# Products of quarters: two outputs computed in place, in the tile of the sum whose last use they are

## The chip, the cores and the metric

The kernel runs on one core of a Trainium2 chip. The metric is the device time of one execution in microseconds (us). Before the change it is 3474.56 us, the median of three runs (3472.7 to 3475.61). Engines are named as in the profile: PE (TensorE), DVE (VectorE), ACT (ScalarE), POOL (GpSimd) and SP (SyncE, which here only issues DMAs).

## The reference

A two-layer backbone over 1024 latent tokens and 256 context tokens, D = 1024. The change touches only how some input projections are computed:

```
qa, ka, va, za, qb, kb, vb, ob, zb, g = _split_cols(h @ w_in, AB_SIZES)   # layer 0
...
    qb, kb = _axial_rope(qb), _axial_rope(kb)                             # latent tokens only
...
q, f_fwd, f_bwd, i, z = _split_cols(h @ w_in, C_SIZES)                    # layer 1
...
(o.reshape(o.shape[:2] + (HG_VW,)) * jax.nn.silu(z)) @ w_out
```

In layer 0 the products concerned are h @ w_in for three pairs of heads: q of heads 0 and 1, k of heads 0 and 1, k of heads 2 and 3 (with the rotation `_axial_rope` for the latent tokens). In layer 1 they are the columns of i (the values) and of z, of which silu(z) is kept.

## The kernel before, in words

**Products of quarters.** `q_seven` (from line 961) multiplies a matrix h (quarters 11, 12, 21, 22: two halves of the tokens by two halves of D) with a 2 x 2 block of weight columns by seven products of quarters in place of eight, in this order: 11 and 12 (`q_two`, line 953), s1, s2, s3, 22, s4, where s1 to s4 use sums of quarters of h. Each quarter product is done in fp32r with a split into a high and a low part, so each 128x256 block takes 12 matmuls (lines 127, 128, 129: high by high, low weight by high, high weight by low). Two running sums live in SBUF tiles: u (names qu, q_keep, line 941) and v (names qv). u is started by the product 11 (copied by ACT, line 957), enlarged by s2 (line 969) and s3 (line 974), and last used in the product 22. v is made from s1 and u (line 971), and last used in the product s4.

**The four outputs.** `q_out` (lines 948 to 951) takes a new output tile, lets DVE add or subtract a product in PSUM to or from the sum (line 950, one instruction per unit), and gives the tile to a sink. There are four calls: the output of the product 12 (reads u), of s3 (reads v), of 22 (last use of u) and of s4 (last use of v). The output tiles rotate: in layer 0 two buffers named ev (shared with the projections before and after the stage), in layer 1 three buffers named qo.

**Sinks.** In layer 0 the sink rotates q and k in place (`rope`, lines 1018 to 1021: four DVE instructions per unit, with a scratch tile qs; units of context tokens are not rotated) and stores the tile to DRAM (line 981, a DMA issued by POOL; md is the place in DRAM). In layer 1 the values go to DRAM at once (line 981, into vd), and for z ACT computes a sigmoid into qg (line 991), DVE multiplies in place (line 992) and POOL issues the store (line 994, into zd).

**Units and buffers.** A product is cut into units, each with a PSUM bank (names sa, mm, tr; eight banks in all). Layer 0: half = 5 blocks of 128 tokens, units of 1, 2 and 2 blocks (128x256, 128x512, 128x512), two sets of u and one set of v. Layer 1: half = 4, two units of 128x512, one set of u and one of v. Layer 0 has three blocks of columns through `q_seven` (the first two have their `q_two` done ahead, `a_ahead`, from line 1028), layer 1 has seven.

**Weights.** `q_form` forms sums of raw weight quarters on DVE (line 899) and splits them: ACT casts the high part (wh, line 74), DVE subtracts for the low part (wl, line 75); each of wh and wl has four buffers. After the stage of layer 0 the neighbourhood attention begins: `na_qk` takes weights through the same buffers and lines, projects (lines 127 to 129 into mm), copies the bank to an ev tile (ACT, line 565) and goes on from there. Its second set of weights, for `na_z`, is in SBUF space that the tiles of the stage (u, v, qs among them) had.

**What sets the order.** A scheduler orders the instructions of each engine ahead of time. On the chip each engine runs its list in order; where a tile is not free yet, the instruction that wants it waits, and all behind it on the engine wait too. In the whole-run trace the stage of layer 0 lies at about 284 to 450 us, that of layer 1 at about 1915 to 2190 us.

Of the kernel before, what the change touches and what calls it, by code (L numbers as in the profile page):

```python
# [9 lines left out]
F32 = mybir.dt.float32  # L10
# [3 lines left out]
ALU = mybir.AluOpType  # L14
# [4 lines left out]
P = 128  # L19
# [27 lines left out]
class Prog:  # L47
# [897 lines left out]
    def q_keep(self, pool, tag, m):  # L945
        return self.t(pool, [P, m * 256], F32, f"{tag}{m}", self.qn * sum(x[1] == m for x in self.units))

    def q_out(self, sink, r, c, u, in0, in1, op):
        o = self.t(self.qo[0], [P, 512], F32, *self.qo[1:])[:, 0 : u[1] * 256]
        self.nc.vector.tensor_tensor(out=o, in0=in0, in1=in1, op=op)  # L950
        sink(c, r * self.half + u[0], u[1], o)

# [9 lines left out]
    def q_seven(self, raw, S, sink, pool, u=None, tr=False):  # L962
        tt = self.nc.vector.tensor_tensor
        u = u or self.q_two(raw, S, sink, pool, tr)
        v, m5 = {}, {}
        for i, ps in self.q_product("s1", S, self.q_form(raw, "11", "12"), tr):
            m5[i] = ps
        for i, ps in self.q_product("s2", S, self.q_form(raw, "11", "22"), tr):
            tt(out=u[i], in0=u[i], in1=ps, op=ALU.add)
            v[i] = self.t(pool, [P, i[1] * 256], F32, f"qv{i[1]}", sum(x[1] == i[1] for x in self.units))  # L970
            tt(out=v[i], in0=m5[i], in1=u[i], op=ALU.subtract)
        for i, ps in self.q_product("s3", S, self.q_form(raw, "12", "22"), tr):
            self.q_out(sink, 1, 1, i, v[i], ps, ALU.subtract)
            tt(out=u[i], in0=u[i], in1=ps, op=ALU.add)
        for i, ps in self.q_product("22", S, self.q_form(raw, "11", "21"), tr):
            self.q_out(sink, 1, 0, i, u[i], ps, ALU.add)
        for i, ps in self.q_product("s4", S, self.q_form(raw, "22"), tr):
            self.q_out(sink, 0, 1, i, v[i], ps, ALU.add)

    def q_store(self, dst, t, m, o):  # L980
        self.nc.gpsimd.dma_start(
# [686 lines left out]
```

## Time and profile before

| | |
|---|---|
| median of three runs | 3474.56 us (3472.7 to 3475.61) |
| the profiled execution | 3477.65 us; span in its trace 3475.9 us; mean granted TensorE clock 0.996 |
| instructions in the span | 63362 |
| DMA | 359.62 MB, mean 103 GB/s |
| chain that ended last, by engine | PE 88%, issue 4%, DMA 2%, DVE 2%, ACT 1%, POOL 1% |

The span is the stretch from the first to the last profiled instruction; the execution's time has 1.75 us more around it. "Busy" of PE counts the time in which at least one matmul is in flight: a 128x256 matmul is shown with 0.28 us, but one starts every 0.12 us, so PE's idle time is read from the distance of starts, not from the busy share. A row of a timeline has the start, the duration, the engine, the line, the operation and the tiles, and in brackets the idle time of the engine just before it and what ended it. A row of waits has who waited for whom, the total in us, how many times, and the longest.

### The profile page before, as it was taken

How to read it: one execution, taken by the hardware profiler on the slowest of the kernel's cores; microseconds unless marked ns; L12 is line 12 of the kernel's file. 1: busy time of each engine (PE TensorE's matmuls, PEld its weight loads, DVE VectorE, ACT ScalarE, POOL GpSimd, SP SyncE). 2: the span in 40 equal slices, each digit the busy share in tenths (PEclk: the TensorE clock that was granted, in tenths of full speed). 3: DMA queues.
4: the chain of work that ended last, by engine and by line, in shares of the span. 5: the costliest groups of instructions: out<-in, count | busy, mean ns of one | idle time of the engine just before them, and what ended most of it. 6: DMA issues, size and time to landing. Idle time of an engine off the chain costs nothing.

```text
span 3475.9 us, 63362 instructions
## 1 busy us (share of the span) xinstructions
PE 3433.5 (99%) x23790; PEld 3111.0 (90%) x23790; DVE 2393.0 (69%) x5876; ACT 1554.2 (45%) x3560; POOL 508.8 (15%) x843
## 2 busy tenths in 40 slices
PE   8999999999999999999999999999999999999999
PEld 6899999999999999988879998889999999999887
DVE  7569857766666654666668766577777777777855
ACT  6532135555545534566536323444444444444431
POOL 3211111222222211211212111000000000000010
PEclk9999999999999999999999999999999999999999
DMA  8542422332222234455475332212111111121345
GB/s 256 165 158 84 124 83 54 91 87 69 81 82 79 75 99 152 128 172 159 131 238 171 101 104 97 82 31 62 62 47 52 58 58 49 52 61 53 113 149 166
DMA packets 354131, 359.62 MB, mean 103 GB/s; under 512 B 30312, under 2 KB 298792, under 8 KB 353696
## 3 DMA queue, kind: packets, MB, share of 16 engines
q1 hardware_dynamic: 309760, 246.28, 24.0%
q0 software_dynamic: 43920, 109.16, 9.2%
q8 instruction: 188, 3.08, 0.4%
q14 instruction: 119, 0.97, 0.1%
q10 hardware_dynamic: 144, 0.13, 0.0%
HBM read 271.90 MB, written 83.42 MB: 102 GB/s over the span
## 4 chain that ended last, share of the span: by engine, by line
PE 88%; issue 4%; DMA 2%; DVE 2%; ACT 1%; POOL 1%; SPq 0%; POOLq 0%; DVEq 0%; ACTq 0%
PE mm L127 15%; PE mm L128 15%; PE mm L129 15%; PE s L1144 6%; PE mm L757 3%; PE mm L759 3%; PE mm L758 3%; PE acc L709 2%; PE tr L689 2%; PE sa L127 2%; PE sa L129 2%; PE sa L128 2%; PE acc L492 2%; PE s L499 2%; PE s L1190 1%
## 5 line engine op out<-in xcount | busy, mean ns | idle before, releaser
L128 PE MATMUL mm<-wl,hh 128*128 128x256 f32 x2200 | 633.0, 288 | 4.0 <-DVE wl L75 3.7
L127 PE MATMUL mm<-wh,hh 128*128 128x256 f32 x2200 | 632.4, 288 | 4.3 <-DVE ev L950 2.7
L129 PE MATMUL mm<-wh,hl 128*128 128x256 f32 x2200 | 632.2, 288 | 0.2 <-DVE hl L75 0.2
L129 PE MATMUL mm<-hh,wl 128*128 128x512 f32 (+1 forms) x1372 | 499.7, 364 | 0.0
L128 PE MATMUL mm<-hl,wh 128*128 128x512 f32 (+1 forms) x1372 | 495.6, 361 | 0.0
L127 PE MATMUL mm<-hh,wh 128*128 128x512 f32 (+1 forms) x1372 | 495.2, 361 | 0.0
L127 PEld LDWEIGHTS mm<-wh,hh 128*128 128x128 f32 x2200 | 420.5, 191 | 12.3 <-issue 6.9
L128 PEld LDWEIGHTS mm<-wl,hh 128*128 128x128 f32 x2200 | 420.9, 191 | 9.4 <-DVE wl L75 5.0
L129 PEld LDWEIGHTS mm<-wh,hl 128*128 128x128 f32 x2200 | 420.5, 191 | 4.1 <-issue 0.8
L74 ACT CAST wh<-wraw 128x512 fp32r<-128x512 f32 x292 | 180.0, 621 | 280.1 <-PE mm L128 147.2
L128 PEld LDWEIGHTS mm<-hl,wh 128*128 128x128 f32 x1372 | 259.3, 189 | 32.2
L127 PEld LDWEIGHTS mm<-hh,wh 128*128 128x128 f32 x1372 | 259.4, 189 | 32.1
L129 PEld LDWEIGHTS mm<-hh,wl 128*128 128x128 f32 x1372 | 259.2, 189 | 32.0 <-issue 0.2
L1135 ACT COPY gksel<-gK 128x512 f32<-128x512 f32 x224 | 148.3, 663 | 275.7 <-PE s L1144 264.6
L75 DVE TENSOR_TENSOR wl<-wraw,wh 128x512 fp32r<-128x512 f32 x292 | 198.5, 688 | 50.5 <-ACT wh L74 47.9
L1144 PE MATMUL s<-gQ,gksel 128*128 128x128 f32 x1536 | 202.1, 276 | 0.0
L1144 PEld LDWEIGHTS s<-gQ,gksel 128*128 128x128 f32 x1536 | 192.6, 191 | 5.8
L757 PE MATMUL mm<-woh,yh 128*128 128x512 f32 (+1 forms) x420 | 168.9, 402 | 4.1 <-issue 2.3
L758 PE MATMUL mm<-wol,yh 128*128 128x512 f32 (+1 forms) x420 | 167.1, 399 | 0.0
L759 PE MATMUL mm<-woh,yl 128*128 128x512 f32 (+1 forms) x420 | 166.2, 397 | 0.1
L1165 DVE TENSOR_TENSOR gQ<-gQ,gT 128x256 f32<-128x256 f32 x384 | 143.9, 417 | 21.3 <-PE s L1144 21.3
L74 ACT CAST wh<-b 128x512 fp32r<-128x512 f32 x122 | 75.7, 620 | 182.3 <-PE sa L129 56.4
(551 smaller groups left out, 8240.4 us busy)
## 6 DMA issues: line engine op xcount, KB each, us to landing
wraw<-in_wc_dram SPq DMA_DIRECT2D x130, 256.0 KB
wraw<-yd SPq DMA_DIRECT2D x128, 256.0 KB
wraw<-in_wab_dram SPq DMA_DIRECT2D x98, 256.0 KB
md<-ev POOLq DMA_DIRECT2D x94, 256.0 KB, 2.7
adar<-in_wada_dram POOLq DMA_DIRECT2D x32, 512.0 KB, 5.0
b<-in_wc_dram SPq DMA_DIRECT2D x62, 256.0 KB
adar<-in_wada_dram SPq DMA_DIRECT2D x16, 512.0 KB
wraw<-in_wab_dram SPq DMA_DIRECT2D x64, 128.0 KB
```

The lines of the kernel that those rows point to most:

```text
L74: nc.scalar.copy(hi, x)
L75: nc.vector.tensor_tensor(out=lo, in0=x, in1=hi.bitcast(F32), op=ALU.subtract)
L127: mm(ps, lhsT=lh(k), rhs=rh(k), start=(first and k == 0), stop=False)
L128: mm(ps, lhsT=lh(k), rhs=rl(k), start=False, stop=False)
L129: mm(ps, lhsT=ll(k), rhs=rh(k), start=False, stop=(last and k == nk - 1))
L492: nc.tensor.matmul(num, lhsT=qc[:, j, :], rhs=C[d][:, j, :], start=False, stop=(j == 1))
L757: mm(ps, lhsT=yh[:, k, :], rhs=w.h(k)[:, cols], start=(k == 0), stop=False)
L758: mm(ps, lhsT=yh[:, k, :], rhs=w.l(k)[:, cols], start=False, stop=False)
L759: mm(ps, lhsT=yl[:, k, :], rhs=w.h(k)[:, cols], start=False, stop=(k == 7))
L1135: nc.scalar.copy(ksel.rearrange("p (b s i) -> p b s i", s=2, i=h), pick(K))
L1144: nc.tensor.matmul(pa[:, c, :].rearrange("p (b s i) -> p b s i", s=2, i=h), lhsT=ksel[:, c * P : (c + 1) * P], rhs=qp[:, c * nbc : (c + 1) ...
L1165: nc.vector.tensor_tensor(out=t[:, i, :, s, :], in0=t[:, i, :, s, :], in1=bc(tot), op=ALU.mult)
```

## The change

```diff
-    def q_out(self, sink, r, c, u, in0, in1, op):
-        o = self.t(self.qo[0], [P, 512], F32, *self.qo[1:])[:, 0 : u[1] * 256]
+    def q_out(self, sink, r, c, u, in0, in1, op, o=None):
+        if o is None:
+            o = self.t(self.qo[0], [P, 512], F32, *self.qo[1:])[:, 0 : u[1] * 256]
         self.nc.vector.tensor_tensor(out=o, in0=in0, in1=in1, op=op)
         sink(c, r * self.half + u[0], u[1], o)
...
         for i, ps in self.q_product("22", S, self.q_form(raw, "11", "21"), tr):
-            self.q_out(sink, 1, 0, i, u[i], ps, ALU.add)
+            self.q_out(sink, 1, 0, i, u[i], ps, ALU.add, u[i])
         for i, ps in self.q_product("s4", S, self.q_form(raw, "22"), tr):
-            self.q_out(sink, 0, 1, i, v[i], ps, ALU.add)
+            self.q_out(sink, 0, 1, i, v[i], ps, ALU.add, v[i])
```

The outputs of the products 22 and s4 no longer take an ev (layer 0) or qo (layer 1) tile: DVE writes them into the tile of u or v, and the rotation, the sigmoid's product and the store work on that tile. The outputs of 12 and s3 are as before. No instruction is added or removed; but half of the takers of ev and qo are gone, a tile of u or v is free again only when its store has landed, and the scheduler, which sees these other waits, orders the stage of layer 0 anew. In layer 1 the order is the same, with other tile names. All lines from 949 on have a number higher by one in the changed kernel (950 becomes 951, and so on).

**Place 1, DVE in the stage of layer 0, around the output of the product 22 of the first block.** Names: qu_515 is the third unit of u of that block, mm_3838 (before) and mm_3836 (after) is the PSUM bank with its product 22, qv_578 and qv_580 are units of v, ev are output tiles, wl the low parts of weights, mrope the table of the rotation. Before:

```order
L1020 TENSOR_TENSOR ev_3797<-ev_3797,qs_3799 128x2x64
L1021 TENSOR_TENSOR ev_3797<-ev_3797,qs_3799 128x2x64
L1018 TENSOR_TENSOR qs_3832<-ev_3830,mrope_2103 128x512
L1019 TENSOR_TENSOR ev_3830<-ev_3830,mrope_2103 128x512
L75 TENSOR_TENSOR wl_4133<-b_622_3969,wh_4134 128x512
L1020 TENSOR_TENSOR ev_3830<-ev_3830,qs_3832 128x4x64
L1021 TENSOR_TENSOR ev_3830<-ev_3830,qs_3832 128x4x64
L75 TENSOR_TENSOR wl_4138<-b_623_3971,wh_4139 128x512
L969 TENSOR_TENSOR qu_538_3357<-qu_538_3357,tr_4060 128x256
L950 TENSOR_TENSOR ev_3863<-qu_515_3231,mm_3838 128x512
L950 TENSOR_TENSOR ev_3887<-qv_576_3621,sa_3874 128x256
L1018 TENSOR_TENSOR qs_3889<-ev_3887,mrope_2103 128x256
```

After, on the same engine at the same place:

```order
L1019 TENSOR_TENSOR qs_3798<-qu_511_3177,mrope_2103 128x256
L951 TENSOR_TENSOR qv_578_3649<-qv_578_3649,sa_3891 128x512
L1020 TENSOR_TENSOR ev_3736<-ev_3736,mrope_2103 128x512
L951 TENSOR_TENSOR ev_3770<-qv_580_3677,tr_3745 128x512
L975 TENSOR_TENSOR qu_515_3231<-qu_515_3231,tr_3745 128x512
L75 TENSOR_TENSOR wl_4045<-wraw_3955,wh_4046 128x512
L1020 TENSOR_TENSOR qu_511_3177<-qu_511_3177,mrope_2103 128x256
L75 TENSOR_TENSOR wl_4050<-wraw_3957,wh_4051 128x512
L1021 TENSOR_TENSOR ev_3736<-ev_3736,qs_3738 128x4x64
L1022 TENSOR_TENSOR ev_3736<-ev_3736,qs_3738 128x4x64
L951 TENSOR_TENSOR qv_580_3677<-qv_580_3677,sa_3923 128x512
L951 TENSOR_TENSOR qu_515_3231<-qu_515_3231,mm_3836 128x512
```

The row that reads the product 22 out of the bank mm (third unit) stood behind the rotations of the units before it and behind the weights of the next block's s3 (wl_4133, wl_4138); now it stands ahead of both, right behind the weights of s2 (wl_4045, wl_4050).

**Place 2, PE at the end of the stage of layer 0.** mm_5086 (before) and mm_5068 (after) are the first projection of `na_qk`, mm_5143 (after) its second; wh_5053/wl_5052 to wh_5074/wl_5073 (before) and wh_5035/wl_5034 to wh_5056/wl_5055 (after) are its four pieces of weights. Before, the rows from the tenth matmul of the first projection on:

```order
L127 MATMUL mm_5086<-wh_5060,hh_128 128x256
L128 MATMUL mm_5086<-wl_5059,hh_128 128x256
L129 MATMUL mm_5086<-wh_5060,hl_129 128x256
L127 MATMUL mm_5086<-wh_5067,hh_128 128x256
L128 MATMUL mm_5086<-wl_5066,hh_128 128x256
L129 MATMUL mm_5086<-wh_5067,hl_129 128x256
L127 MATMUL mm_5086<-wh_5067,hh_128 128x256
L128 MATMUL mm_5086<-wl_5066,hh_128 128x256
L129 MATMUL mm_5086<-wh_5067,hl_129 128x256
L127 MATMUL mm_5086<-wh_5074,hh_128 128x256
L128 MATMUL mm_5086<-wl_5073,hh_128 128x256
L129 MATMUL mm_5086<-wh_5074,hl_129 128x256
```

After, the rows from the 18th matmul after s4 on (ahead of them 12 of mm_5068 and 5 of mm_5143, all with the first two pieces of weights):

```order
L129 MATMUL mm_5143<-wh_5035,hl_129 128x256
L127 MATMUL mm_5143<-wh_5042,hh_128 128x256
L128 MATMUL mm_5143<-wl_5041,hh_128 128x256
L127 MATMUL mm_5068<-wh_5049,hh_128 128x256
L129 MATMUL mm_5143<-wh_5042,hl_129 128x256
L127 MATMUL mm_5143<-wh_5042,hh_128 128x256
L128 MATMUL mm_5143<-wl_5041,hh_128 128x256
L129 MATMUL mm_5143<-wh_5042,hl_129 128x256
L127 MATMUL mm_5143<-wh_5049,hh_128 128x256
L128 MATMUL mm_5068<-wl_5048,hh_128 128x256
L129 MATMUL mm_5068<-wh_5049,hl_129 128x256
L127 MATMUL mm_5068<-wh_5049,hh_128 128x256
```

The second projection is begun ahead of the end of the first: the low part of the third piece of weights was wanted by the 14th matmul after s4 and is now wanted by the 27th.

**Place 3, ACT at the same end.** wh_5462 (before) and wh_5444 (after) is the first weight tile in SBUF space that the stage gives back; ev_5135 and ev_5117 are the copies of the first projection of `na_qk`. Before:

```order
L74 CAST wh_5074<-wraw_5075 128x512
L74 CAST wh_5462<-wraw_5463 128x512
L74 CAST wh_5468<-wraw_5469 128x512
L565 COPY ev_5135<-mm_5086 128x512
L569 ACTIVATE aqn_5137<-ev_5135 128x512
```

After:

```order
L74 CAST wh_5056<-wraw_5057 128x512
L565 COPY ev_5117<-mm_5068 128x512
L74 CAST wh_5444<-wraw_5445 128x512
L74 CAST wh_5450<-wraw_5451 128x512
L569 ACTIVATE aqn_5119<-ev_5117 128x512
```

The copy that frees the bank of the first projection now stands ahead of the cast into space of the stage, instead of behind it. That cast waited for the last rotation (line 1021); now it waits for the landing of the last store of v, too.

## The prediction

> **What bounds the kernel now.** I read the page first, for the engine that is always busy and for what makes it wait; then the stretches of the two stages; then the waits inside the first; then the rows around them.
>
> ```profile
> PE 3433.5 (99%) x23790; PEld 3111.0 (90%) x23790; DVE 2393.0 (69%) x5876; ACT 1554.2 (45%) x3560; POOL 508.8 (15%) x843
> L127 PE MATMUL mm<-wh,hh 128*128 128x256 f32 x2200 | 632.4, 288 | 4.3 <-DVE ev L950 2.7
> ```
>
> PE bounds the run, so only a change of PE's waits or clock moves the time. One of its few waits is on line 950, which the change edits. The stretches (their columns: us, then busy us and count of PE, PEld, DVE, ACT and POOL, the granted clock, DMA share, GB/s):
>
> ```profile
> 316.00:360.00 44.00, 41.62 (x347) 41.19 (x347) 38.44 (x79) 7.46 (x12) 7.98 (x12) 1.00 0.40 120
> 360.00:405.00 45.00, 45.00 (x381) 45.00 (x379) 39.44 (x82) 9.37 (x16) 8.02 (x12) 1.00 0.24 77
> 405.00:450.00 45.00, 39.82 (x315) 39.44 (x314) 33.56 (x66) 6.08 (x11) 8.87 (x14) 0.93 0.50 153
> 1915.00:1990.00 75.00, 75.00 (x480) 68.13 (x479) 55.94 (x90) 25.95 (x42) 9.00 (x14) 1.00 0.31 102
> ```
>
> In layer 0 (first three rows) PE has holes, and in the third row its clock is below 1. In layer 1 (last row) it has neither: there the change can cost, but not gain. In layer 0 the waits say who:
>
> ```profile
> DVE ev L950 <- DMA md<-ev: 16.2, 10, 3.1
> PE mm L127 <- DVE ev L950: 4.8, 2, 2.7
> PE mm L128 <- DVE wl L75: 2.7, 2, 2.5
> ```
>
> DVE stands still ten times, 16.2 us in all, because both ev tiles are still being stored. PE waits twice for line 950 (a PSUM bank not read out) and once at length for a low part of weights, which DVE makes too. The three holes of PE, each with the row before it and the row that ends it:
>
> ```profile
> 353.80 0.28 PE L129 MATMUL tr<-wh,s2l 128*128 128x256 f32 x1
> 356.24 0.36 PE L127 MATMUL mm<-wh,s2h 128*128 128x256 f32 x1 [2.16 <-DVE ev L950]
> 435.47 0.28 PE L127 MATMUL mm<-wh,hh 128*128 128x256 f32 x1
> 438.27 0.38 PE L128 MATMUL mm<-wl,hh 128*128 128x256 f32 x1 [2.52 <-DVE wl L75]
> 441.72 0.28 PE L129 MATMUL mm<-wh,hl 128*128 128x256 f32 x1
> 444.66 0.55 PE L127 MATMUL mm<-wh,hh 128*128 128x256 f32 x1 [2.66 <-DVE ev L950]
> ```
>
> **The sum, term by term.** A 128x256 matmul starts 0.12 us after the one before where nothing waits, so a hole costs the distance of starts less 0.12. Rows from DVE's timeline and from the chain (start, duration, engine, line) give the causes:
>
> ```profile
> 338.48 0.42 DVE L1018 TENSOR_TENSOR qs<-ev,mrope 128x256 f32<-128x256 f32 x1
> 351.47 0.29 DVE L1020 TENSOR_TENSOR ev<-ev,qs 128x128 f32<-128x128 f32 x1
> 351.67 0.29 DVE L1021 TENSOR_TENSOR ev<-ev,qs 128x128 f32<-128x128 f32 x1
> 354.14 0.42 DVE L1021 TENSOR_TENSOR ev<-ev,qs 128x256 f32<-128x256 f32 x1
> 354.48 0.68 DVE L75 TENSOR_TENSOR wl<-b,wh 128x512 fp32r<-128x512 f32 x1
> 355.41 0.68 DVE L950 TENSOR_TENSOR ev<-qu,mm 128x512 f32<-128x512 f32 x1
> 436.92 0.69 DVE L950 TENSOR_TENSOR ev<-qu,sa 128x512 f32<-128x512 f32 x1 [2.77 <-DMA md<-ev]
> 437.53 0.69 DVE L75 TENSOR_TENSOR wl<-wraw,wh 128x512 fp32r<-128x512 f32 x1
> ```
>
> ```profile
> 441.24 2.56 DMA md<-ev
> 443.82 0.70 DVE ev L950
> 445.21 0.21 PE mm L128
> 450.54 0.21 PE mm L129
> 452.22 0.12 PE mm L127
> ```
>
> *Hole 1, 356.24 - 353.80 - 0.12 = 2.32 us.* PE wants the bank mm; line 950 reads it out only at 355.41, though DVE did not wait: it had other rows first. In the new order (place 1) the row with mm_3836 stands nearer. From the row of 338.48, which both orders have, to that row there are now 16 rows of 512 columns (0.61 us apart, as 436.92 and 437.53), 8 that are 256 wide or two halves of a 512 rotation (0.34 apart, as 354.14 and 354.48), 2 narrow ones (0.2 apart, as 351.47 and 351.67) and its own 0.68: 9.8 + 2.7 + 0.4 + 0.7 = 13.6, so it ends at about 352.1. PE wants the bank at 353.92. The hole goes, with 1.8 us to spare.
>
> *Hole 2, 438.27 - 435.47 - 0.12 = 2.68 us.* The low part of the fourth piece of weights (437.53) stood behind a row of line 950 that waited 2.77 us for an ev store. That row now writes into u, which is free. What is late next: the same low parts behind the output of s4's last unit. Place 2 shows the third piece wanted by the 27th matmul after s4, 3.1 us after its end; DVE needs from that end one output row, two halves of a rotation and the two low parts, 0.61 + 0.68 + 1.22 = 2.5 us. So no hole there, with 0.6 us to spare.
>
> *Hole 3, 444.66 - 441.72 - 0.12 = 2.82 us.* The chain shows the whole of it: a store lands (441.24, 2.56 us), DVE writes into the ev tile (443.82), PE gets its bank. With v written in place no store stands before line 951. It goes whole.
>
> *The clock.* Behind hole 3 matmuls are 0.21 apart (445.21 to 450.54), later 0.12 again (452.22). From 444.66 to the end of that stretch at 450.76 lie 6.10 us, in which 29 matmuls start; at 0.12 they take 3.5. Loss 2.6 us, which goes if PE is not idle before it.
>
> [...] The trace speaks for the hole, since the low clock begins with it; but the row with hole 1, of 2.32 us, has a clock of 1.00, so a hole of that size is not always followed by it.
>
> Sum: 2.32 + 2.68 + 2.82 + 2.6 = 10.4 us.
>
> *Does DVE hold out?* It has the same instructions, and in place costs nothing more:
>
> ```profile
> L974 DVE TENSOR_TENSOR qu<-qu,sa x12: 412/680/690, 336.8 to 2099.1; 128x512 f32<-128x512 f32 x10, 128x256 f32<-128x256 f32 x2
> L950 DVE TENSOR_TENSOR ev<-qu,sa x7: 415/680/687, 290.0 to 438.1; 128x512 f32<-128x512 f32 x4, 128x256 f32<-128x256 f32 x3
> ```
>
> Both medians are 680 ns, the first with u as output and input. From 316 to 450 us DVE is busy 38.44 + 39.44 + 33.56 = 111.4 us and PE starts 1043 matmuls, 125.2 us at 0.12. So without PE's holes DVE is at 89%: close, but still the second.
>
> *The waits that are added.* A tile of u or v is free only when its store has landed:
>
> ```profile
> L981 POOL DMA_DIRECT2D md<-ev x36: 562/707/727, 316.0 to 449.9; - x36
> DMA to landing us min/median/max: 2.0/2.6/8.6
> ```
>
> That is 0.71 + 2.6 = 3.3 us from the last rotation. The tightest place is the second block's v (line 972 after the change), with the low parts of later weights and the outputs of s3 queued behind it on DVE: between the last rotation of a unit of v and the row that rewrites it the new order has 10 rows: two rotation halves of a 512 unit and two 256-wide sums (4 x 0.34), two 256-wide rotations that wait for each other (2 x 0.42, their whole duration), two narrow halves (2 x 0.2) and two low parts (2 x 0.61), 3.8 us together. So 0.5 us to spare in the median case. A landing of 8.6 us would cost DVE 5.5. The third block's v has a whole `q_two` in between, the u of layer 0 two sets. In layer 1, the last stores of a z block and the copies of the next block that rewrite u:
>
> ```profile
> 1985.35 0.54 POOL L994 DMA_DIRECT2D zd<-qo  x1 [1.86 <-DVE qo L992]
> 1989.03 0.54 POOL L994 DMA_DIRECT2D zd<-qo  x1 [3.14 <-DVE qo L992]
> 1994.12 0.59 ACT L957 COPY qu<-tr 128x512 f32<-128x512 f32 x1 [1.06 <-PE tr L129]
> 1997.00 0.59 ACT L957 COPY qu<-mm 128x512 f32<-128x512 f32 x1
> ```
>
> With 0.54 + 2.6 us the stores land at 1988.5 and 1992.2: 5.6 and 4.8 us early. Cost of layer 1: nothing, cover 4.8 us per block.
>
> *The end of the stage.* ACT's cast into returned space waits for v's last store too:
>
> ```profile
> 449.65 1.14 ACT L74 CAST wh<-wraw 128x512 fp32r<-128x512 f32 x2 [15.52 <-DVE ev L1021]
> 450.70 0.58 ACT L565 COPY ev<-mm 128x512 f32<-128x512 f32 x1
> ```
>
> Behind it stand the other casts and the copies of the banks, but the first copy now stands ahead (place 3), so PE has two banks in hand. After s4 DVE needs 2.5 us as above and 1.9 for the last rotation (2 x 0.61 + 2 x 0.34), the store 3.3: it lands about 8 us after s4, when PE is still in its first 96 matmuls, which take 11.5. Cost nothing.
>
> One residue: two large loads (hh, hl, line 1047) pass through POOL's queue in the third block, in the new order right behind two ev stores instead of ahead of them. A store that lands late there can hold line 951 and with it PE; I put it between 0 and 1 us, and take 0.4, since the stores are issued first. So 10.0 us.
>
> **From the profiled execution to the median.** The profiled execution took 3477.65 us, 1.75 more than its span, and 3.1 more than the median of the runs shown. A hole of PE is the same in both, so I take 10.0 off the median: 3474.56 - 10.0 = 3464.6 us.
>
> **The rivals.**
>
> 1. *DVE takes PE's place.* At 89% with an order in which a row may wait for PE, part of the holes can come back elsewhere: for it speaks hole 1, where DVE was late without any wait; against it the spare time at each bank (1.8 and 0.6 us the least). If one hole of 2.3 to 2.8 us and the low clock after it stay, 4.9 to 5.4 are left out of 10.0: about 3469.7 us.
>
> 2. *The low clock stays.* What holds it may be the phase of its switching and not the hole. Then 10.0 - 2.6 = 7.4: 3467.2 us. [...]
>
> 3. *Nothing to be seen.* If the new order keeps DVE behind PE by as much as before, the saved store waits become waits of DVE for PE, and the time is 3472 to 3476 us. Against it: holes 2 and 3 end in rows that hang on ev stores by name.
>
> 4. *Slower: the tiles are held by their stores.* Place: line 972 in the second block of layer 0 (queued: low parts and outputs), and line 958 at the seven block ends of layer 1 (queued on ACT: the casts). Price at a landing of 8.6 us: 5.5 in layer 0; in layer 1 the second copy's store would land at 1989.03 + 0.54 + 8.6 = 1998.2, 1.2 us late, 7 x 1.2 = 8.4; with two stretches of low clock 5.2 more. 3464.6 + 19.1 = 3483.7 us. It decides from landings of about 7.4 us on in layer 1; the median is 2.6, and I expect a landing of that size only behind the two large loads of the third block, so it is unlikely.
>
> That the change does not do what it says: the orders show that it does, the tiles qu and qv are what is stored.
>
> **How the numbers follow.** Forecast (all three holes and the low clock gone) 0.62; rival 1 0.16; rival 2 0.06; rival 3 0.10; rival 4 0.06. A measurement of this kernel tells about 0.2%, 6.9 us, from no change, so faster means below 3467.6. The forecast's own range is 3462 to 3467.5 (spare time of DVE, the residue, and a stretch of low clock elsewhere more or less). Faster: 0.62 + 0.06 for rival 2, less 0.02 for its edge, 0.66. Rivals 1 and 3 are within 0.2%, with that edge 0.28. Slower 0.06. The range takes in rivals 1 and 2: 3461.5 to 3471.0 us; outside are rivals 3 and 4, 0.16, and little more.
>
> **What would show it.** In the profile of the changed kernel: the row of DVE's line 951 waiting for md falls from 16.2 us to under 3; PE has no hole over 1 us between 325 us and the attention; the stretch from 405 us on has a clock of 1.00; the end of s4 comes about 2.3 us earlier, and the matmul that started at 450.76 about 10 us earlier. Wrong would be: a new wait of DVE's line 972 or ACT's line 958 for a store, a hole of PE at a bank that DVE reads out late, or idle PE in 1915 to 2190 us.

## The result, and the profile after

The changed kernel takes 3466.36 us (median of 15 runs, 3461.18 to 3472.91), the kernel before beside it 3476.34 us (15 runs, 3472.7 to 3480.63). The ratio is 0.9973, with a 95% interval of 0.9965 to 0.9981. The medians differ by 9.98 us; 10.0 was forecast. The time itself is 1.8 us above the forecast of 3464.6, because the kernel before has a median of 3476.34 over 15 runs and 3474.56 in the three runs that the forecast started from.

First the page of the changed kernel, with the two rows that stood at the head of the prediction:

```profile
PE 3430.0 (99%) x23790; PEld 3112.2 (90%) x23790; DVE 2390.0 (69%) x5876; ACT 1553.9 (45%) x3560; POOL 512.6 (15%) x843
...
L127 PE MATMUL mm<-wh,hh 128*128 128x256 f32 x2200 | 633.1, 289 | 1.2 <-ACT wh L74 1.1
```

The work is the same (counts and busy times), but PE's idle time ahead of line 127 fell from 4.3 to 1.2 us, and DVE's output row is no longer what ended most of it. The stretches of the two stages (us, busy us and count of PE, PEld, DVE, ACT and POOL, granted clock, DMA share, GB/s):

```profile
316.00:360.00 44.00, 43.78 (x369) 43.51 (x368) 41.50 (x88) 7.65 (x13) 8.49 (x13) 1.00 0.38 116
360.00:405.00 45.00, 45.00 (x380) 45.00 (x379) 40.05 (x84) 9.96 (x17) 10.09 (x16) 1.00 0.30 96
405.00:450.00 45.00, 45.00 (x381) 45.00 (x380) 32.52 (x66) 9.32 (x17) 11.05 (x15) 1.00 0.57 175
1915.00:1990.00 75.00, 75.00 (x475) 67.93 (x475) 53.26 (x85) 25.46 (x41) 9.30 (x15) 1.00 0.33 109
```

From 360 to 450 us PE is busy without a hole, and at full clock in the third row, where it had 39.82 of 45 us and 0.93. In the first row 0.22 us are left, a hole that both kernels have at about 326 us. DVE gets a little more done in the same time. The waits of DVE from 284 to 445 us, from the longest on (who waits for whom, us in total, times, longest), and then all of PE's:

```profile
DVE wl L75 <- ACT wh L74: 10.8, 9, 4.5
DVE wraw L899 <- DMA wraw<-in_wab_dram: 1.8, 2, 1.3
DVE ar L571 <- ACT aqn L569: 1.7, 1, 1.7
DVE qu L970 <- PE mm L129: 1.1, 1, 1.1
```

```profile
PE mm L128 <- DVE wl L75: 0.2, 1, 0.2
```

What matters here is what is missing. "ev <- md", 16.2 us and the first row before, is gone altogether, and no row of line 972 waits for a store. The wait of line 75 for ACT is longer than before (4.1), which costs PE nothing.

All kernels here execute the same 23,790 matmuls, so the start of the matmul with the same number can be compared between traces. From number 1980 (294.12 us before, 294.79 after) to number 3564 (499.12 and 488.97) lies **the stage of layer 0 with its end: 205.00 us before, 194.18 after**. The difference grows in three steps: 2.58 us at hole 1, 2.76 at hole 2, and 5.55 at hole 3 with the low clock behind it. From number 13860 to 15840 lies **layer 1's stage: 323.73 us in both**. These two lengths carry the comparisons below, because the whole time also holds stretches of low clock (0.50) elsewhere, which differ from run to run (mean clock 0.996 to 0.999 in the 15 runs of the changed kernel): outside the stage they begin at 20.63, 37.69, 1498.60, 3393.00 and 3474.92 us in the profile of the kernel before, at 38.73, 48.97, 1270.94, 1489.40, 3243.85 and 3462.30 in that of the changed one.

### The profile page after: what moved, and what is told of

Its sections match the earlier page's. It is cut to its first block, busy times and chain, and to the rows that moved or that the text cites. A ratio compares the mean times of both kernels' runs of the same rounds, so it can differ in the third digit from the quotient of the medians.

```text
span 3464.8 us, 63394 instructions
## 1 busy us (share of the span) xinstructions
PE 3430.0 (99%) x23790; PEld 3112.2 (90%) x23790; DVE 2390.0 (69%) x5876; ACT 1553.9 (45%) x3560; POOL 512.6 (15%) x843
## 5 line engine op out<-in xcount | busy, mean ns | idle before, releaser
L1158 DVE COPY_PREDICATED gA<-glm,s 128x512 f32<-128x512 uint8 x160 | 117.1, 732 | 55.8 <-PE s L1145 55.8
```

The costliest lines, as they stand in the source:

```text
L1158: nc.vector.copy_predicated(A, self.lmask[:, lev - 1, :].unsqueeze(1).to_broadcast([P, 4, P]), pa)
```

## The experiments

| kernel | stage of layer 0, us | median, us | ratio to before, 95% interval |
|---|---|---|---|
| before | 205.00 | 3476.34 | |
| changed | 194.18 | 3466.36 | 0.9973 (0.9965 to 0.9981) |
| e1, layer 0 alone | 194.30 | 3466.22 | 0.9962 (0.995 to 0.9974) |
| e2, layer 1 alone | 203.76 | 3477.2 | 0.9997 (0.9989 to 1.0006) |
| e3, u alone | 194.14 | 3465.91 | 0.9967 (0.9955 to 0.998) |
| e4, v alone | 194.15 | 3468.3 | 0.9969 (0.9957 to 0.9981) |
| e5, four output tiles, nothing in place | 193.57 | 3467.29 | 0.9967 (0.9956 to 0.9978) |
| e11, control for e5, two tiles | 202.47 | 3477.98 | 0.9999 (0.999 to 1.0007) |
| e7, stores issued twice | 194.13 | 3464.68 | 0.996 (0.9948 to 0.9972) |
| e9, projections in turn | 194.90 | 3470.04 | 0.9975 (0.9965 to 0.9985) |
| e6, 18 more rows of DVE | 196.41 | 3470.49 | 0.9979 (0.9971 to 0.9988) |
| e6, 36 more rows of DVE | 204.66 | 3480.84 | 1.0002 (0.9993 to 1.0011) |
| e8, 6 to 30 rows in a block of layer 1 | 194.11 | 3501.84 (one run) | |
| e10, 13 to 16 rows in a block of layer 1 | 194.20 | 3468.06 (one run) | |

The ratios from e1 on are to runs of the kernel before on the same chip, with medians of 3477.45 to 3477.94 us. Five or more runs stand behind each ratio.

**Which layer (e1, e2).**

```diff
-            self.q_out(sink, 1, 0, i, u[i], ps, ALU.add, u[i])
+            self.q_out(sink, 1, 0, i, u[i], ps, ALU.add, u[i] if self.qo[1] == "ev" else None)
```

and the same for v[i] (e1); with "qo" in place of "ev" it is e2.

> In place only in layer 0; layer 1 keeps its three qo tiles. Theory (the whole gain is three holes of PE and the low clock behind the third, all in layer 0): about 10 us below the kernel before (ratio 0.997), no row of DVE's line 951 waiting for a store, no hole of PE over 1 us between 325 us and the attention. Rival (a good part of the gain comes from layer 1, where half of the takers of qo are gone): clearly less, 5 us or under.

> In place only in layer 1; layer 0 is as before. Theory: no change, within 2 us of the kernel before, the three holes of 2.3 to 2.8 us still there, and PE without a hole in the stage of layer 1, as in both kernels. Rival (layer 1 gives part of the gain): 3 to 8 us below. What it also shows: whether the low clock comes again behind the third hole. If the hole is its cause, it comes in this profile too; if the phase of its switching decides, it may be missing here, or stand behind another hole.

e1 has the whole gain and e2 none. Layer 1's stage takes 323.73 us in each of them. e2 also has the three holes again, and its waits read as those of the kernel before did:

```profile
DVE ev L951 <- DMA md<-ev: 16.5, 10, 3.7
PE mm L127 <- DVE ev L951: 4.9, 2, 2.7
```

The gain is layer 0's, all of it.

**Which output (e3, e4).** In e3 the call for v has lost its last argument, in e4 the call for u:

```diff
-            self.q_out(sink, 0, 1, i, v[i], ps, ALU.add, v[i])
+            self.q_out(sink, 0, 1, i, v[i], ps, ALU.add)
```

> Only the output of the product 22 is written in place (into u), in both layers; the output of s4 takes an ev or qo tile. Theory (each hole belongs to the output whose row stood still: hole 2 to the third block's row of u, hole 3 to the last row of v): hole 2 goes, hole 3 of about 2.8 us stays, hole 1 (an order of rows) probably goes with the new order; some 5 us below the kernel before, 4 to 6 us above the changed one. Rival (two ev tiles are enough once any output leaves them): the whole 10 us.

> Only the output of s4 is written in place (into v), in both layers; the output of the product 22 takes an ev or qo tile. Theory (each hole belongs to the output whose row stood still): hole 3 and the low clock behind it go, about 5.5 us; hole 2 (2.7 us) stays, since the six rows of s3 and of the product 22 still share two ev tiles; hole 1 open. Some 5 to 8 us below the kernel before. Rival (two ev tiles are enough once any output leaves them): the whole 10 us.

The theory fell and its rival stands: either half gives the whole, 194.14 and 194.15 us. DVE's waits for output tiles are not even gone. The row in e3, and then in e4:

```profile
DVE ev L951 <- DMA md<-ev: 2.9, 3, 2.0
```

```profile
DVE ev L951 <- DMA md<-ev: 6.1, 4, 2.6
```

In e4 DVE stands still for up to 2.6 us at a time, and the only wait of PE in the stage is again 0.2 us for line 75. A store that held DVE cost time here only where DVE had no lead on PE. With a quarter fewer takers of the two ev tiles, and the order that the scheduler makes of it, the lead is there at all three places. Which output belonged to which hole did not matter.

**Tiles, or writing in place (e5, e11).** All four outputs as before, but from four tiles:

```diff
-    def q_out(self, sink, r, c, u, in0, in1, op):
-        o = self.t(self.qo[0], [P, 512], F32, *self.qo[1:])[:, 0 : u[1] * 256]
+    def q_out(self, pool, sink, r, c, u, in0, in1, op):
+        self.no = getattr(self, "no", 0) + 1
+        home = (pool, "eo", 2) if self.no % 2 and self.qo[1] == "ev" else self.qo
+        o = self.t(home[0], [P, 512], F32, *home[1:])[:, 0 : u[1] * 256]
...
-        self.ropet = self.t(pool, [P, 2, 8, 2, 64], F32, "mrope", 1)
+        self.ropet = self.t(pool, [P, 1, 8, 2, 64], F32, "mrope", 1)
```

e11 has only the smaller table, without the four tiles.

> The kernel before, nothing in place, but four output tiles in layer 0 in place of two (two ev and two of a name eo, taken in turn). To make room, only one of the two tables of the rotation is loaded and used for both products: the same instructions, other values. Theory (what costs is the wait for an output tile, in place or not): about 10 us below the kernel before, no wait of DVE for a store over 1 us, no hole of PE over 1 us from 325 us on. Rival (it is the writing into u and v, and the order that follows from it, that helps): at least one hole of 2 us stays, 5 us or less below.

> The control for the run with four output tiles: the kernel before, with two, where only one of the two tables of the rotation is loaded and used for both products (other values, the same instructions in the same order). Theory (the four tiles made the gain there): no change, within 2 us of the kernel before, the three holes are there. Rival (the smaller load makes the gain): about 10 us below. It is also a third profile of the same three holes, at another place in the grid of the clock's stretches: by the rule of idle time in a stretch of 3.41 us, the low clock behind hole 3 lasts for two stretches, one or none, and costs about 1.3 us for each.

The stretches of e5:

```profile
316.00:360.00 44.00, 44.00 (x374) 44.00 (x374) 41.03 (x85) 8.70 (x14) 8.58 (x13) 1.00 0.42 124
360.00:405.00 45.00, 45.00 (x380) 45.00 (x380) 41.35 (x88) 8.90 (x15) 10.82 (x16) 1.00 0.31 99
405.00:450.00 45.00, 45.00 (x381) 45.00 (x380) 31.57 (x63) 11.49 (x21) 11.13 (x16) 1.00 0.53 164
```

With nothing in place there is no hole at all: even that at about 326 us is gone, which is most of the 0.6 us by which the stage is shorter than in the changed kernel (193.57 against 194.18), too little for the medians to tell. The control has the three holes and no gain (ratio 0.9999). What cost the time was the shortage of output tiles; writing in place is one way to end it, and its merit is that it takes no space.

This also corrects the reading of hole 1. There DVE had not waited, and the prediction put the hole down to the order of the rows. The kernel before, POOL's store of the tile that the late row takes again, and DVE's row that had filled it:

```profile
352.26 0.57 POOL L981 DMA_DIRECT2D md<-ev  x1 [3.32 <-DVE ev L1021]
```

```profile
349.02 0.43 DVE L950 TENSOR_TENSOR ev<-qu,mm 128x256 f32<-128x256 f32 x1
```

For that store the profile gives 2.0 us to its landing. Such a time counts from the start of the issue, not from its end, as the next store and the row that waits for it show (3.8 us to landing):

```profile
354.86 0.71 POOL L981 DMA_DIRECT2D md<-ev  x1 [2.03 <-DVE ev L1021]
```

```profile
358.73 0.42 DVE L950 TENSOR_TENSOR ev<-qv,sa 128x256 f32<-128x256 f32 x1 [2.63 <-DMA md<-ev]
```

354.86 + 3.8 = 358.66, just ahead of 358.73. At hole 3 it is the same: the store of 441.24 takes 2.56 us to land, and the row that takes its tile starts at 443.82. So the store of 352.26 landed at 352.26 + 2.0 = 354.26. The row that PE waited for started at 355.41: with the tiles of the kernel before, an earlier place could have brought it forward by 1.15 us at the most, half of the hole. Until 354.26 its tile was not free, and the rows that stood ahead of it filled a wait that would have shown otherwise.

**Tile or new order at hole 2 (e9).** The interleaved projections of place 2 are undone, with the tiles of the changed kernel:

```diff
-            for j in range(2):
-                self.proj_nat(ps[:, j, :], w, tt + j, 0, 256)
+            with self.tc.issue_after(last) if p2 == 0 and tt == 2 else nullcontext():
+                for j in range(2):
+                    self.proj_nat(ps[:, j, :], w, tt + j, 0, 256)
+            last = nc.cur_bb.bb.instructions[-1]
```

> The changed kernel with one rule of order more: at the end of the stage of layer 0 PE does the second projection of na_qk only behind the first, as in the kernel before; the tiles are as in the changed kernel. If the free tile alone closes hole 2, there is no hole here and no change. By the prediction's step on hole 2, DVE needs 2.5 us from the end of s4 to the low part of the third piece, which PE now wants again with the 14th matmul, 1.6 us after that end: a hole of about 0.9 us at line 128, and some 1 us above the changed kernel, so that 1.8 us of hole 2's 2.68 are the tile's and 0.9 the new order's.

PE's and DVE's rows at that place in e9:

```profile
433.05 0.28 PE L127 MATMUL mm<-wh,hh 128*128 128x256 f32 x1
433.82 0.39 PE L128 MATMUL mm<-wl,hh 128*128 128x256 f32 x1 [0.50 <-DVE wl L75]
```

```profile
432.75 0.41 DVE L1024 TENSOR_TENSOR qv<-qv,qs 128x256 f32<-128x256 f32 x1
433.09 1.28 DVE L75 TENSOR_TENSOR wl<-wraw,wh 128x512 fp32r<-128x512 f32 x2
```

A hole of 433.82 - 433.05 - 0.12 = 0.65 us opens at the third piece of weights, six matmuls ahead of hole 2's place, where 0.9 was worked out, and the stage is 0.72 us longer. The low parts start at 433.09 straight behind the rotation, with no store in between. So the free tile is worth about 2.0 of hole 2's 2.68 us, and the new order the other 0.65. The median is 3.7 us above the changed kernel's, but the ratios to before on the same chip are nearly the same (0.9975 and 0.9973), and beyond 0.7 us nothing in the stage explains more.

**The tiles held longer (e7).** Each store of u and v in layer 0 is issued twice:

```diff
-            self.q_store(dst[c], t, m, o)
+            for _ in range(2 if (c == 0) == (t >= 5) else 1):
+                self.q_store(dst[c], t, m, o)
```

> The changed kernel with each store of a u or v tile in layer 0 issued twice, so that those tiles come free later by about 0.7 us. Forecast (tiles of v have about 0.5 us to spare in the second block, u has two sets): DVE's line 972 shows waits for a store of a few tenths, the time stays within 1 us of the changed kernel. Rival 4 (tiles held by their stores): waits of over 2 us on lines 972 or 970, a hole of PE, 3 us or more above the changed kernel.

The second store of a tile waited for the first to land, and POOL's queue with it (2.83 us in the second row below), so the tiles were held longer than expected. The two stores of the first unit of v, and DVE's row that rewrites it in the second block:

```profile
358.12 0.57 POOL L982 DMA_DIRECT2D md<-qv  x1
361.52 0.71 POOL L982 DMA_DIRECT2D md<-qu  x1 [2.83 <-DMA md<-qu]
362.23 0.57 POOL L982 DMA_DIRECT2D md<-qv  x1
```

```profile
366.17 0.42 DVE L972 TENSOR_TENSOR qv<-sa,qu 128x256 f32<-128x256 f32 x1 [2.53 <-DMA md<-qv]
```

The tile is held for 8 us from its first store on, DVE stands still for 2.53 us at the very row that rival 4 named, and PE shows no hole: the stage takes 194.13 us. Rival 4's place was right and its price wrong, since DVE's lead on PE takes it up. The test is not quite of the same order: the scheduler, which sees the second stores, puts this row four rows later than in the changed kernel. In the changed kernel itself, the stores of the second and third unit of v and the row that rewrites the second:

```profile
364.86 1.43 POOL L982 DMA_DIRECT2D md<-qv  x2 [4.76 <-DVE qv L1022]
```

```profile
369.07 0.68 DVE L972 TENSOR_TENSOR qv<-tr,qu 128x512 f32<-128x512 f32 x1
```

The first of those two stores lands 2.6 us after its start at 364.86, at 367.4: 1.6 us to spare, where 0.5 was worked out.

**More work for DVE (e6).** The first row of a rotation runs two or three times for the outputs of the first half of the tokens:

```diff
-        tt(out=v4(s), in0=v4(o), in1=tab(1), op=ALU.mult)
+        for _ in range(2 if home == self.qsr and t < 5 else 1):
+            tt(out=v4(s), in0=v4(o), in1=tab(1), op=ALU.mult)
```

> The changed kernel with 18 more rows of DVE in the stage of layer 0: the first row of the rotation runs twice for the outputs of the first half of the tokens, 6 x 0.34 + 12 x 0.61 = 9.4 us more for DVE. Forecast (PE is still the bound, DVE at 89% has room): within 1.5 us of the changed kernel, about 3467 us or 9 below the kernel before. Rival 1 (DVE is about to take PE's place): 5 to 9 us of the gain are lost, holes of PE come back at banks that DVE reads out late.

> As the run with 18 more rows of DVE, with 36: 18.8 us more work of DVE in the stage of layer 0. With 18 rows the stage lost 2.3 us. If DVE is now the bound of the stage, each further us costs about one: 8 to 12 us above the changed kernel. If only single rows are late (a hole here and there), the loss is about twice that of 18 rows: 4 to 6 us.

With 18 rows (9.4 us) the stage is 2.2 us longer than the changed kernel's, more than the 1.5 us of the forecast and less than rival 1 asks; with 36 (18.8 us) it is 10.5 us longer, the size that was expected of a bound DVE (8 to 12). But most of it stands in one row of PE, the same in both runs; first 18 rows, then 36:

```profile
345.50 0.39 PE L127 MATMUL sa<-wh,s4h 128*128 128x256 f32 x1 [1.66 <-DVE qu L975]
```

```profile
350.53 0.58 PE L127 MATMUL sa<-wh,s4h 128*128 128x256 f32 x1 [6.89 <-DVE qu L975]
```

That is the start of s4 in the first block, where DVE still has outputs of the two `q_two` to rotate; with 36 rows two stretches of low clock follow the hole of 7.05 us (mean clock 0.92 from 316 to 360 us). With 36 rows it is not load alone: rotations that take longer hold the ev tiles longer, and DVE waits for stores again, twice ahead of that row (1.57 and 1.45 us):

```profile
DVE ev L951 <- DMA md<-ev: 4.1, 3, 1.6
```

Behind the hole, with 36 rows still:

```profile
351.00:435.00 84.00, 84.00 (x691) 84.00 (x691) 77.50 (x163) 16.32 (x27) 16.13 (x24) 0.97 0.39 120
```

DVE is at 92% (77.50 of 84), and PE has no further hole. So 9 us more found room on DVE nearly everywhere, and at one place did not. Rival 1's mechanism is real; it begins beyond the load of this change.

**The clock (e8, e10, with the profiles of before, e2 and e11).** DVE rows put in ahead of a sum in layer 1, from block to block more of them (self.nb counts the blocks; here e8, while e10 has 13 to 16 rows in each):

```diff
+            for _ in range(6 + 4 * (self.nb - 3) if self.nb > 3 and i[0] == 0 else 0):
+                tt(out=u[i], in0=u[i], in1=u[i], op=ALU.max)
```

> The changed kernel with rows put in to make holes of PE in layer 1: ahead of the first sum of s2 in each of its seven blocks DVE takes the maximum of u with itself 6, 10, 14, 18, 22, 26 and 30 times (0.6 to 0.7 us each, no change of values). PE runs some banks ahead, so the first blocks may show no hole and the last ones holes up to about 10 us. Theory (the clock is set for fixed stretches of 3.41 us by how much PE was idle in the stretch before; about 1.6 to 1.9 us of idle time are enough): holes of 2 to 4 us are followed by the low clock or not depending on where they lie in that grid, holes over 5 us always. [...]

> The changed kernel with holes of PE made in layer 1 as in the run with 6 to 30 rows, now with 13, 15, 14, 13, 16, 14 and 15 rows of DVE in the seven blocks, for holes between 1 and 5 us. Theory (the clock of a stretch of 3.41 us is set by PE's idle time in the stretch before it, low from about 1.6 to 1.9 us on): holes of 2.5 to 4 us have the low clock behind them where one stretch holds over 1.9 us of them, none where they are cut in two parts under 1.6. [...]

e10 made no hole: layer 1's stage takes 323.72 us, and on the clock it says nothing. e8 made holes of 0.99, 2.20, 6.36, 8.49 and 10.19 us, the clock low behind the last three only (0.96 in the mean from 1905 to 2260 us); none lay between 2.5 and 5, so on the length alone it decides little. But the records of the clock show something sharper. It changes only at times that lie multiples of 3.41 us apart (the low stretches of the kernel before last 3.41 us, as 20.63 to 24.04, or 6.83, as 37.69 to 44.52 and 443.88 to 450.71), and the stretches of that grid, taken one by one, show what goes ahead of a low one. The kernel before, hole 1 in the first two rows and holes 2 and 3 in the next two:

```profile
351.72:355.13 3.41, 2.36 (x20) 2.15 (x19) 3.38 (x9) 1.24 (x2) 0.84 (x2) 1.00 0.39 123
355.13:358.55 3.42, 2.31 (x19) 2.34 (x20) 0.96 (x3) 0.00 (x0) 1.16 (x2) 1.00 0.88 283
437.05:440.47 3.42, 2.20 (x18) 2.20 (x19) 3.35 (x6) 0.00 (x0) 0.71 (x1) 1.00 0.30 77
440.47:443.88 3.41, 1.53 (x13) 1.32 (x12) 2.29 (x8) 0.00 (x0) 0.72 (x1) 1.00 0.45 157
443.88:447.29 3.41, 2.63 (x12) 2.66 (x13) 3.17 (x6) 0.00 (x0) 0.57 (x1) 0.50 0.11 38
447.29:450.71 3.42, 3.42 (x18) 3.42 (x17) 2.67 (x6) 1.06 (x3) 1.43 (x2) 0.50 0.22 77
```

e2, the same holes at another place in the grid, hole 3 in the first row:

```profile
443.11:446.52 3.41, 1.18 (x10) 0.97 (x9) 2.27 (x7) 0.00 (x0) 0.89 (x2) 1.00 0.34 118
446.52:449.94 3.42, 2.99 (x14) 3.02 (x15) 3.15 (x7) 0.00 (x0) 0.41 (x1) 0.50 0.11 38
449.94:453.35 3.41, 3.41 (x30) 3.41 (x30) 2.66 (x6) 1.38 (x3) 1.44 (x2) 1.00 0.27 89
```

e11, again the same order of instructions, hole 1 in the first row and hole 2 in the second:

```profile
352.33:355.75 3.42, 1.69 (x15) 1.51 (x14) 2.44 (x6) 0.15 (x1) 1.38 (x2) 1.00 0.48 133
...
434.25:437.67 3.42, 1.22 (x11) 1.09 (x10) 2.44 (x4) 0.00 (x0) 0.25 (x1) 1.00 0.27 76
437.67:441.08 3.41, 3.41 (x19) 3.41 (x18) 2.36 (x7) 0.00 (x0) 1.18 (x2) 0.50 0.57 179
441.08:444.49 3.41, 2.24 (x19) 2.07 (x19) 3.03 (x7) 0.00 (x0) 0.57 (x1) 1.00 0.25 88
```

A stretch at full clock in which PE was busy 1.53 (45%), 1.22 or 1.18 us of 3.41 has a low one behind it; after 1.69, 2.20, 2.31 or 2.36 us the clock stayed at 1.00. A stretch that is low already is another matter: in the kernel before the one at 443.88, with PE busy 2.63 us, has a second low one behind it, in e2 the one at 446.52, with 2.99 us, has none. The same hole of 2.4 to 2.8 us therefore brings two low stretches, one or none, as it lies in the grid, and in e11 it is hole 2 that has one. The stage of the kernel before takes 205.00 us (two low stretches behind hole 3), 203.76 (one) and 202.47 in these three profiles. In the last, PE ran slowly ahead of hole 3, and its two late rows there are these:

```profile
442.98 0.36 PE L127 MATMUL mm<-wh,hh 128*128 128x256 f32 x1 [1.17 <-DVE ev L950]
```

```profile
449.64 0.39 PE L127 MATMUL mm<-wh,hh 128*128 128x256 f32 x1 [0.67 <-ACT ev L565]
```

Of hole 3 there are 1.33 us left (441.53 to 442.98, less 0.12), and 0.83 us come back at the next bank (448.69 to 449.64, less 0.12): ACT's copy of it stands behind the cast into returned space, the order that place 3 showed for the kernel before.

## Why the prediction was right, step by step

*PE bounds, and layer 1 can only lose.* Right. Layer 1's stage is 323.73 us with the change and without it (e1, e2).

*Hole 1, 2.32 us.* The size was right (2.58 with the slow start behind it), the cause half right: the row did stand late, but it could not have stood more than 1.15 us earlier, because its tile was still being stored. In the changed kernel it stands ahead, as place 1 showed:

```profile
351.87 0.67 DVE L951 TENSOR_TENSOR qu<-qu,mm 128x512 f32<-128x512 f32 x1
```

It ends at 352.54. The stage began 0.67 us later in this profile and ran 0.06 us longer up to here (the hole at about 326 us), so that is 351.8 on the clock of before, where 352.1 was worked out. The new order also has PE begin the bank sa there before it goes on to mm, which the prediction did not see. That is not what closed the hole: in e3 PE takes the banks in the order of before (last into tr at 353.64, first into mm at 353.76) and has no hole either.

*Hole 2, 2.68 us.* It went whole (2.76). The remark that the low parts have 0.6 us to spare, given the new order, is borne out by e9: without that order 0.65 us are missing, and the new order wants the piece 13 matmuls later, 1.6 us, so that some 0.9 are to spare.

*Hole 3, 2.82 us.* It went, but the reason given asks for more than was needed. "With v written in place" was not needed: with u alone in place it goes too (e3), while DVE still waits 2.0 us for a store somewhere.

*The clock, 2.6 us.* Right for the profiled execution: hole 3 and the clock are 5.55 us there, 5.42 forecast. As a term for the median it was the least certain, since it depends on where the hole lies in the grid. The mean of the three profiles that have this stage as before is (205.00 + 203.76 + 202.47) / 3 = 203.74 us, 9.6 us above the changed kernel's 194.18, not 10.8. Rival 2, that the phase decides, was therefore no true rival: it takes hole and phase together. The time alone could not have told it from the forecast, since its 7.4 us lie inside the interval of the gain; the profiles tell. In the ten whose stage has no hole over 1.9 us no stretch there is low, and in the four others (before, e2, e11 and 36 more rows) one or two are.

*DVE holds out.* Right at this load: 41.50 + 40.05 + 32.52 = 114.1 of 134 us from 316 to 450. The share over the whole stage was a poor measure of the margin, as the one row of PE in e6 shows.

*The added waits.* Right: none shows in the changed kernel. What was missed is that a wait of DVE here need not reach PE, as in e4 (2.6 us) and e7 (2.53 us), so rival 4's price was far too high. It was also too high by its own rows, because the prediction counted the issue twice: the 2.6 us to landing hold it already, so a tile is held 2.6 us from the start of its store and not 0.71 + 2.6 = 3.3. With that the tightest place has 3.8 - 2.6 = 1.2 us to spare in place of 0.5 (1.6 were measured), and rival 4's 19.1 us become about 14 (4.8 + 4.4 + 5.2). The forecast does not change by it.

*The residue, 0.4 us.* It is not to be seen; line 951 waits for no ev store at all.

*What would show it.* The matmul that started at 450.76 (number 3202) starts 10.17 us earlier:

```profile
440.58 0.28 PE L128 MATMUL mm<-wl,hh 128*128 128x256 f32 x1
```

s4's last matmul starts at 431.35 in place of 433.19. That is 1.85 us earlier, where 2.3 was said: hole 1's 2.58 less the 0.73 by which this profile was late ahead of it. The clock is 1.00 from 405 us on, and no hole over 1 us is left.

So the sum of 10.4 - 0.4 = 10.0 us was close to the 9.98 of the medians, partly because a clock term somewhat too large for the mean run stood against terms that came out slightly larger than forecast. That it agrees to 0.02 us is luck: the interval of the ratio stands for a gain of 6.6 to 12.2 us. The span of the profiled execution fell by 11.1 us, from 3475.9 to 3464.8: 10.8 in the stage, 1.0 behind it, less 0.7 by which the stage began later.

What stays open: DVE's new order and the freed tiles always came together but at the place of e9, so how holes 1 and 3 would divide between them was not measured. For hole 1 the landing at 354.26 only sets a bound: order alone could have saved at most 1.15 of 2.32 us.

## What to carry to other kernels

Where an engine that feeds the bound waits for a rotating tile, count the takers of the ring: each relief tried here that restored its lead (one output or two written in place, or more tiles) gave the same gain (a stage of 193.57 to 194.30 us in place of 205.00), and the cheapest one in space is to be had by writing into an operand at its last use. A row that stands late without waiting may stand there because its tile is not free: compare its start with the landing of the store that frees its tile, counted from the start of that store's issue, before calling it an order. A lead is spent at one place, so read the margin of a second engine from its tightest stretch and not from its mean share, and price a low clock behind a hole as a mean over where the hole can fall (here the stage took 205.00, 203.76 and 202.47 us with the same three holes).

## What the runs showed of the hardware that was not expected

In the 128x256 matmuls of this stage the granted clock fell for the next 3.41 us after a stretch of 3.41 us at full clock in which PE was busy 1.53 us or less, and not after 1.69 us or more (before, e2 and e11); hole 3, at 2.82 us, is shorter than such a stretch. Elsewhere in the kernel the edge is not that sharp: in the kernel before, a stretch with 1.60 us of busy PE (from 1682.92 us) has no low one behind it, and one with 1.69 us (from 3389.59 us) has. With one low stretch less the same stage took 1.24 us less (205.00 and 203.76), though its holes differ a little too, and the same holes drew two in one profile and one in another. Under the low clock matmuls started 0.21 us apart in place of 0.12 (from 445.21 to 450.54 us in the kernel before), so PE wants its operands later, and the low stretch ahead of hole 3 in e11 shortened it: of its 2.82 us, 1.33 were left, and 0.83 came back at another bank. The time of these stores to their landing (2.0 us the least, 2.6 the median, 8.6 the most in the kernel before) counts from the start of their issue, and so holds the issue itself (0.56 to 0.73 us).
